# Moving the gelu and the sums of one pass behind other work, and three more idle products, in a two-layer S5, retention and convolution kernel

## The chip, the cores and the metric

The kernel runs on 1 core of a Trainium2 chip, as one program in one launch. The metric is the device time of an execution in microseconds (us), as the median of several runs. TensorE is called PE here, VectorE DVE, ScalarE ACT, GpSimd POOL and SyncE SP. SP issues nearly all transfers (DMAs), in order, so a transfer whose condition is not met holds up those behind it on SP.

## What is computed

The input x has 1024 frames of 1024 values, in float32. Two layers act on it, each as x + mixer(rmsnorm(x)), with a norm at the end.

```python
# layer 0
u, g_s5, q, k, v, g_ret = split(h @ w_in)
y = gelu(s5_mixer(u))                        # diagonal complex state space, chunks of 64
y = y * sigmoid(y @ glu_w + glu_b) * silu(g_s5)
r = retention(rope(q), rope(k), v)           # 8 heads, dk 64, dv 128; normalised per head
x = x + concat(y, r * silu(g_ret)) @ w_out
# layer 1
a, b, g = split(h @ w_in_c)
c = layernorm(causal_conv31(a * sigmoid(b)) + conv_b)
x = x + (silu(c) * silu(g)) @ w_out_c
out = rmsnorm(x)
```

## The kernel before, in words

Data lie with the features on the 128 partitions and the 1024 frames along the free axis, in two halves of 512. So a matrix of 1024 x 1024 values is eight blocks of 128 features. Every large product is made of three products of a rounded high part and a low part (`mm3`, lines 180 to 182: high weight by high x, high weight by low x, low weight by high x). Weights come in as float32, ACT casts the high part (line 170), and DVE or POOL subtracts it to get the low part (line 171).

`run` goes through three stages.

1. `layer0_front`. PE starts with idle products (lines 271 to 273): products of a matrix of ones, whose result nobody reads, as many as the constant WARM says (9). Meanwhile the first pieces of the weights and of x arrive, ACT makes the high part of x (line 295) and DVE the low part (line 296). Squares of x are summed over the blocks on DVE into `ssum` (line 268). The first GEMM, u0 and u1 (lines 310 to 318), runs over the eight blocks kb of the input dimension; then comes the GEMM of u2, and between its halves the sums over the features of `ssum` by 16 small products (line 443, `ss`). The remaining u blocks, the gates and the state space follow. The state space leaves its result in DRAM (`y_d`).
2. `retention`, a loop over 4 pairs of heads. Each pair makes its k and q (`ret_proj`; line 979 evacuates them as `kraw` and `qraw`, four transfers each swap their halves for the rotation, line 988), its values v (`ret_values`: for pairs 2 and 3, eight blocks v_0 to v_7 of 24 products, lines 1025 to 1027, each evacuated by ACT on line 1028), and its heads (`ret_heads`). A pass of y, `y_pass`, is done once in each pair, for the feature blocks k and k + 4.
3. `layer0_back_and_layer1`: the gated linear unit (GLU) on y, the output projection, the convolution, the last projection and the last norm.

PSUM has 8 banks; the pool that the large products share has three, so a new block of v waits for the evacuation of the block three before it.

The order of the instructions on each engine is decided by a scheduler, which runs a model of the timeline when the kernel is built. The source orders it in two ways: `issue_after(x)` adds an edge, so that what is made in it is ordered behind x; and a `yield` in a generator splits a step into parts which the caller starts at a place of its choice.

`y_pass(rq, pair)` is such a generator. For each of its two blocks it loads `yp` from `y_d` (line 878; one buffer, which the high parts of the same pass, `th`, also use), applies gelu on ACT (line 881, the first of each pass with a table load) into `yn` (two buffers) and stores that to `yn_d` (line 883). Four DVE operations, the sums (lines 888 to 891), then combine the halves of the two blocks in place. They are ordered behind `last_raw`, the last evacuation of k or q, and must wait for the stores to `yn_d`, whose data they overwrite. A `yield` follows. The last part casts each block to a high part `th` (line 895), subtracts it in place (line 896) and stores both to `t_d` (lines 897 and 898). These t_d sums, and similar sums of the GLU's weights (`glu_sums`, stored to `ws_d`), let the GLU use fewer products.

In `ret_heads`, k is transposed into `kt` (line 1066, DVE on 1068), kt times v gives the states' increments `kv` (line 1085), DVE runs the recurrence over the chunks into `S` (lines 1093 and 1095), PE makes the scores `sp` (line 1102), DVE multiplies them with the decay mask into `sc` (line 1108), and PE adds `ro` = q times S (line 1129) and sc times v (line 1134). The norm per head (lines 1143 to 1149), a transpose back (`rt`, line 1157) and the gate (line 1160) end the pair. The last of the four mask products is kept as `masked[1]`.

In the loop of `retention`, before the change, the first part of `y_pass` (loads, gelus, stores and sums) is started ahead of `ret_heads`, behind the `rs` of the pair before; in pairs 1 and 2 the rest (casts and stores to t_d) is started behind `masked[1]`. In pair 2 the second gelu is ordered behind `last_v`, the evacuation of the eighth value block; the first gelu has no such edge. In pair 3 all is started ahead of the heads.

Behind the pass of pair 3, the loads `y11f` and `y21f` (line 1191) bring the blocks of yn back for the GLU, and ACT casts them (line 1167, `y11h`).

Of the kernel before, what the change touches and what calls it, by code (L numbers as in the profile page):

```python
# [26 lines left out]
CONV_K = 31  # L27
MAGIC = 12582912.0
N0, HOLD = 5, 1
WARM = 9  # L30
RMM = 5
IDLE = 4
TWICE = ("wo", "cb", "ca", "cg")
# [18 lines left out]
class Trunk:  # L52
# [190 lines left out]
    def layer0_front(self, st):  # L243
# [27 lines left out]
        idle = self.bank("idle")  # L271
        for _ in range(WARM):
            nc.tensor.matmul(idle[:, :P], self.ones[:], self.ones[:], start=True, stop=True)
# [597 lines left out]
    def y_pass(self, rp, k):  # L871


        nc = self.nc
        yns = []
        for i, cb in enumerate((k, k + 4)):
            yt = rp.tile([P, 8, P], F32, name=f"yp_{cb}", tag="yp", bufs=1)
            nc.sync.dma_start(yt[:], self.y_d[cb].rearrange("i h g m -> (h g) i m"))
            yn = rp.tile([P, P, 8], F32, name=f"yn_{cb}", tag="ynt", bufs=2)
            with self.tc.issue_after(self.last_v.ins) if k == 2 and i else nullcontext():  # L880
                nc.scalar.activation(yn[:], yt[:].rearrange("p i m -> p m i"), AF.Gelu_apprx_tanh)
            yn = yn[:].rearrange("p m i -> p (m i)")
            nc.sync.dma_start(self.yn_d[cb * P:(cb + 1) * P], yn)
            yns.append(yn)
        (b11, b12), (b21, b22) = ((y[:, :HALF], y[:, HALF:]) for y in yns)
        v = nc.vector
        with self.tc.issue_after(self.last_raw.ins):
            v.tensor_tensor(b22, b22, b12, op=ALU.subtract)
            v.tensor_tensor(b12, b12, b11, op=ALU.subtract)
            v.tensor_tensor(b11, b22, b11, op=ALU.add)  # L890
            v.tensor_tensor(b21, b11, b21, op=ALU.subtract)
        yield
        for i in range(2):
            hi = rp.tile([P, T], F32R, name=f"th{i}_{k}", tag="yp", bufs=1)
            v.tensor_copy(hi[:], yns[i])
            v.tensor_tensor(yns[i].bitcast(F32R), yns[i], hi[:].bitcast(F32), op=ALU.subtract)
            nc.sync.dma_start(self.t_d[i, 0, k * P:(k + 1) * P], hi[:].bitcast(F32))
            nc.sync.dma_start(self.t_d[i, 1, k * P:(k + 1) * P], yns[i])
# [20 lines left out]
    def retention(self, st):  # L919
        nc, A = self.nc, self.A  # L920
        rp = self.rp = self.pool("ret", 1, stack=st)
        early = ExitStack()
        rq = self.rq = self.pool("retq", 1, stack=early, side="right")
        self.rk = rq.tile([P, 2, T], F32, name="ropek")
        nc.sync.dma_start(self.rk[:], A["rope_k"])
        self.g128 = rp.tile([P, 4], F32, name="g128")
        nc.sync.dma_start(self.g128[:], A["ret_g128"])
        ahead = None
        for pair in range(4):
            cur = list(ahead or self.ret_proj(pair))[-1]  # L930

            ahead = pair == 1 and self.ret_proj(pair + 1)
            if ahead:
                next(ahead)
            for g, tag in (((0, "swp"), (1, "raw")), (), ((3, "raw"),), ())[pair]:
                self.glu_sums(g, tag)
            if pair == 0:
                V = self.ret_values_wide()
            elif pair > 1:
                V = self.ret_values(pair)  # L940
            with ExitStack() as held:
                if pair:
                    held.enter_context(self.tc.issue_after(self.last_rs.ins))
                parts = self.y_pass(rq, pair)
                next(parts)
                if pair in (0, 3):
                    next(parts, None)

            def turned():
                if pair == 3:  # L950
                    early.close()
                    self.lp = self.pool("l1", side="right")
            self.ret_heads(pair, *cur, V, turned)

            if pair < 3:
                with self.tc.issue_after(self.masked[1].ins):
                    if pair == 0:
                        self.glu_sums(2, "swp")
                    else:
                        next(parts, None)  # L960

    def ret_proj(self, pair):
        nc, A, rp = self.nc, self.A, self.rp
# [48 lines left out]
    def ret_values(self, pair):  # L1012

        nc = self.nc
        wv = [self.wnext(f"v{pair}_{i}") for i in range(2)]
        vt = self.rp.tile([P, 8, 256], F32, name=f"v_{pair}", tag="v", bufs=2)
        for b in range(8):
            ps = self.bank(f"mm_v{pair}_{b}", aux=False)
            h, o = b // 4, (b % 4) * P
            for kb in range(KB):  # L1020
                xh, xl = self.xs[h][kb]
                i, k4 = kb // 4, kb % 4
                wh = wv[i][0][:].rearrange("p (k a) n -> p k (a n)", a=2)[:, k4, :]
                wl = wv[i][1][:].rearrange("p (k a) n -> p k (a n)", a=2)[:, k4, :]
                nc.tensor.matmul(ps[:, :256], xh[:, o:o + P], wh, start=kb == 0, stop=False)
                nc.tensor.matmul(ps[:, :256], xh[:, o:o + P], wl, start=False, stop=False)
                nc.tensor.matmul(ps[:, :256], xl[:, o:o + P], wh, start=False, stop=kb == KB - 1)
            self.last_v = nc.scalar.mul(vt[:, b, :], ps[:, :256], self.Rtok[:, b:b + 1])
        return lambda p, b, hh: vt[:, b, hh * P:(hh + 1) * P]

    def ret_values_wide(self):
# [700 lines left out]
```

## Time and profile before

| | us |
|---|---|
| median of 3 runs | 1191.57 |
| the runs | 1190.52, 1191.57, 1194.78 |
| the profiled execution | 1192.05 |
| its span in the trace | 1190.3 |
| PE busy | 1179.0 |
| DVE, POOL, ACT busy | 848.5, 657.8, 481.3 |

The span is what the trace shows, from the first instruction to the last. It is 1.75 us shorter than the time of the same execution. A row of the timeline reads: start, duration, engine, line and operation, result <- operands by their names without numbers, shapes and types, xcount of instructions that the row holds, and in brackets the idle time of the engine ahead of it, with what ended it. A product's duration reaches into the next one's, since products are pipelined: the pace is read from the starts. The waits give for each pair of waiter and releaser the total, the number and the longest. The stretches give, for a window of the span, the busy time of PE, PE's weight loads, DVE, ACT and POOL, each with its count, then the granted clock, the share of the DMA engines and what they moved.

### The profile page before, as it was taken

To read this page: it belongs to the slowest core of one execution; us is meant where nothing else is said; L and a number is where in the kernel's file an instruction comes from. 1 tells how busy PE (TensorE), PEld (TensorE's weight loads), DVE (VectorE), ACT (ScalarE), POOL (GpSimd) and SP (SyncE) were. 2 spreads that over 40 slices of the span, in tenths; PEclk is the share of its full clock that TensorE was granted. 3 is DMA by queue.
4 is the path that set the end of the run, shared out by engine and by line. 5 is a ranking of instruction groups with operands and counts; after the bars stand their busy time and mean duration, and the time that the engine had idled before them with its cause. 6 is when DMAs were issued, how large, how long until landed. Compare 5 with 4: busy or idle time off the path is not lost.

```text
span 1190.3 us, 17367 instructions
## 1 busy us (share of the span) xinstructions
PE 1179.0 (99%) x6366; PEld 988.1 (83%) x6366; DVE 848.5 (71%) x1452; ACT 481.3 (40%) x706; POOL 657.8 (55%) x448
## 2 busy tenths in 40 slices
PE   9999999999999999999999999999999999999997
PEld 7888888888888888899878888888888888888887
DVE  7975798777427459577769323599999799999533
ACT  6222233222232231333446323546535675434563
POOL 2059999988145354242573110688543567757653
PEclk9999999999999999999999999999999999999999
DMA  9244356555388566769998986756668554357773
GB/s 357 91 140 137 116 159 195 176 168 175 109 279 304 211 218 193 255 207 357 381 323 287 333 271 214 233 192 215 222 234 283 205 192 154 134 177 249 246 257 138
DMA packets 117638, 261.47 MB, mean 220 GB/s; under 512 B 10672, under 2 KB 42288, under 8 KB 116912
## 3 DMA queue, kind: packets, MB, share of 16 engines
q1 hardware_dynamic: 117408, 260.33, 64.7%
q8 instruction: 50, 0.82, 0.3%
q14 instruction: 36, 0.29, 0.1%
q10 hardware_dynamic: 144, 0.03, 0.0%
HBM read 181.48 MB, written 74.65 MB: 215 GB/s over the span
## 4 chain that ended last, share of the span: by engine, by line
PE 49%; DMA 3%; POOL 2%; issue 1%; SPq 0%; ACT 0%; DVE 0%; DVEq 0%; POOLq 0%; ACTq 0%
PE mm_wo L182 5%; PE mm_wo L181 5%; PE mm_wo L180 5%; PE mm_g L180 2%; PE mm_b L182 2%; PE mm_g L182 2%; PE mm_b L180 2%; PE mm_b L181 2%; PE mm_a L180 2%; PE mm_g L181 2%; PE mm_a L181 2%; PE mm_a L182 2%; PE mm_oc L181 2%; PE mm_oc L182 2%; PE mm_oc L180 2%; PE mm_glu L180 1%
## 5 line engine op out<-in xcount | busy, mean ns | idle before, releaser
L1415 DVE SCALAR_TENSOR_TENSOR cv<-u,convw,cv 128x512 f32<-128x512 f32 x398 | 273.6, 750 | 12.8 <-ACT cv L1401 10.5
L1395 POOL TENSOR_TENSOR tp<-tp,tp 128x512 f32<-128x512 f32 x64 | 83.0, 1297 | 43.6 <-ACT tp L1394 42.5
L180 PE MATMUL mm_g<-xh,wh_g 128*128 128x512 f32 x256 | 101.8, 398 | 0.0
L182 PE MATMUL mm_g<-xh,wl_g 128*128 128x512 f32 x256 | 100.1, 391 | 0.0
L181 PE MATMUL mm_g<-xl,wh_g 128*128 128x512 f32 x256 | 100.0, 391 | 0.0
L412 POOL TENSOR_TENSOR s1q<-s1q,s1q 128x512 f32<-128x512 f32 x12 | 17.8, 1481 | 76.8 <-ACT s1q L407 76.8
L1394 ACT ACTIVATE tp<-u,convw 128x512 f32<-128x512 f32 x64 | 45.4, 719 | 31.4 <-POOL tp L1395 31.1
L180 PEld LDWEIGHTS mm_g<-xh,wh_g 128*128 128x128 f32 x256 | 48.0, 188 | 11.7 <-issue 1.2
L182 PEld LDWEIGHTS mm_g<-xh,wl_g 128*128 128x128 f32 x256 | 48.0, 188 | 10.4
L181 PEld LDWEIGHTS mm_g<-xl,wh_g 128*128 128x128 f32 x256 | 48.1, 188 | 9.9 <-issue 0.4
L180 PE MATMUL mm_oc<-zh,wh_woc 128*128 128x512 f32 (+1 forms) x152 | 54.5, 364 | 0.0
L368 DVE TENSOR_TENSOR gt<-mm_g,R 128x512 f32<-128x512 f32 x32 | 21.9, 684 | 45.5 <-PE mm_g L182 45.5
L181 PE MATMUL mm_oc<-zl,wh_woc 128*128 128x512 f32 (+1 forms) x152 | 54.0, 357 | 0.3 <-POOL zl L1169 0.3
L182 PE MATMUL mm_oc<-zh,wl_woc 128*128 128x512 f32 (+1 forms) x152 | 53.8, 357 | 0.0
L171 POOL TENSOR_TENSOR wl_glu<-wf_glu,wh_glu 128x1024 fp32r<-128x1024 f32 x14 | 34.9, 2491 | 31.7 <-ACT wh_glu L170 25.1
L180 PE MATMUL mm_u<-xh,wh_u 128*128 128x512 f32 x128 | 51.3, 401 | 0.6 <-ACT wh_u L170 0.5
L181 PE MATMUL mm_u<-xl,wh_u 128*128 128x512 f32 x128 | 50.6, 395 | 0.0
L180 PE MATMUL mm_g<-h1h,wh_cg 128*128 128x512 f32 x128 | 50.4, 394 | 0.0
L180 PE MATMUL mm_b<-h1h,wh_cb 128*128 128x512 f32 x128 | 50.2, 392 | 0.0
L182 PE MATMUL mm_a<-h1h,wl_ca 128*128 128x512 f32 x128 | 50.2, 392 | 0.0
L182 PE MATMUL mm_u<-xh,wl_u 128*128 128x512 f32 x128 | 50.0, 395 | 0.0
L180 PE MATMUL mm_wo<-ysh,wh_wos 128*128 128x512 f32 x128 | 49.9, 390 | 0.0
(490 smaller groups left out, 3649.6 us busy)
## 6 DMA issues: line engine op xcount, KB each, us to landing
wf_g<-w_ab SPq DMA_DIRECT2D x16, 512.0 KB
wf_wos<-w_out SPq DMA_DIRECT2D x16, 512.0 KB
wf_wor<-w_out SPq DMA_DIRECT2D x16, 512.0 KB
wf_cb<-w_c SPq DMA_DIRECT2D x16, 512.0 KB
wf_ca<-w_c SPq DMA_DIRECT2D x16, 512.0 KB
wf_woc<-w_out_c SPq DMA_DIRECT2D x16, 512.0 KB
wf_v<-w_v SPq DMA_DIRECT2D x12, 512.0 KB
wf_cg<-w_c SPq DMA_DIRECT2D x11, 512.0 KB
```

The costliest lines, as they stand in the source:

```text
L171: lo[i].tensor_tensor(wl[:].rearrange(fl)[:, c], wf[:, c], h.bitcast(F32), op=ALU.subtract)
L180: nc.tensor.matmul(ps, wh[:, kb, :], xh, start=start, stop=False, **more)
L181: nc.tensor.matmul(ps, wh[:, kb, :], xl, start=False, stop=False, **more)
L182: self.last_mm = nc.tensor.matmul(ps, wl[:, kb, :], xh, start=False, stop=stop, **more)
L368: nc.vector.tensor_tensor(gt[:, c], ps[:], self.R[:, c], op=ALU.mult)
L412: nc.gpsimd.tensor_tensor(a, a, sq[:], op=ALU.add)
L1394: nc.scalar.mul(sk[:], u[:, k:k + HALF], cw[:, nb, k:k + 1])
L1395: gp.tensor_tensor(s0[:], s0[:], sk[:], op=ALU.add)
L1415: v.scalar_tensor_tensor(dst[:], *tap, accs_[i][:], op0=ALU.mult, op1=ALU.add)
```

## The change

WARM goes from 9 to 12. In `y_pass` for pair 2, the first gelu is ordered behind `mid_v`, the evacuation of the fifth value block (b == 4), and the second stays behind `last_v`. A new `yield` stands between the gelus and the sums. In `retention`, pairs 0, 1 and 3 call `next` once more, so that their order of parts stays; in pair 2 the sums and the casts are both started behind `masked[1]`, after `ret_heads` has been laid out. Lines of the new file lie two further down from `y_pass` on, and more behind it.

```diff
-WARM = 9
+WARM = 12
...
-            with self.tc.issue_after(self.last_v.ins) if k == 2 and i else nullcontext():
+
+            with self.tc.issue_after((self.last_v if i else self.mid_v).ins) if k == 2 else nullcontext():
                 nc.scalar.activation(yn[:], yt[:].rearrange("p i m -> p m i"), AF.Gelu_apprx_tanh)
             yn = yn[:].rearrange("p m i -> p (m i)")
             nc.sync.dma_start(self.yn_d[cb * P:(cb + 1) * P], yn)
             yns.append(yn)
+        yield
         (b11, b12), (b21, b22) = ((y[:, :HALF], y[:, HALF:]) for y in yns)
...
                 next(parts)
+                if pair != 2:
+                    next(parts)
                 if pair in (0, 3):
                     next(parts, None)
...
                     else:
-                        next(parts, None)
+                        for _ in parts:
+                            pass
...
             self.last_v = nc.scalar.mul(vt[:, b, :], ps[:, :256], self.Rtok[:, b:b + 1])
+            if b == 4:
+                self.mid_v = self.last_v
```

The scheduler orders everything anew. Beside the steps named, the order on the engines changes in these places. On PE the products of u0 and u1 for kb 2 to 5 are sorted by operand, one product of u2's second half goes ahead of the `ss` sums, and some products of k of pair 3 change places with the heads of pair 2. On ACT the cast of a weight block of v3 goes ahead of the gelu of yn_6, and that of the first GLU weight block ahead of the gelu of yn_7. On DVE the sums and casts of pair 2 are interleaved with the norm statistics behind the masks, and the second half of kraw_3 goes ahead of the last cast. On SP the store of yn_2 and the load of yp_6 go behind the gs1_3 and ropeq_3 loads, two ws_d stores, two yr_d stores and a grl load; the store of yn_6 goes behind the second grl load and a GLU weight load; the four kswp transfers of pair 3 go ahead of the load of yp_3; and the second pair of y11f loads directly follows the store of yn_7.

## The prediction

> **What bounds the kernel now.** I read the page first, then the stretches by engine, then TensorE's waits. The page:
>
> ```profile
> span 1190.3 us, 17367 instructions
> PE 1179.0 (99%) x6366; PEld 988.1 (83%) x6366; DVE 848.5 (71%) x1452; ACT 481.3 (40%) x706; POOL 657.8 (55%) x448
> ```
>
> TensorE (PE) is busy for all but 11.3 us of the span. The change takes no real product away, so it can only touch those 11.3 us, or the speed at which the products run. Where the idle lies, by stretches (the first figure after the length is PE's busy time):
>
> ```profile
> 0.00:10.00 10.00, 8.45 (x28) 7.24 (x29) 4.94 (x12) 6.24 (x10) 0.84 (x7) 1.00 0.79 293
> ...
> 60.00:460.00 400.00, 400.00 (x2479) 333.76 (x2479) 263.63 (x427) 109.55 (x167) 279.55 (x187) 1.00 0.57 183
> 460.00:480.00 20.00, 19.53 (x148) 18.34 (x147) 17.14 (x59) 7.04 (x11) 9.24 (x6) 1.00 0.70 210
> 480.00:520.00 40.00, 38.99 (x291) 34.35 (x290) 27.02 (x79) 9.40 (x13) 10.09 (x6) 1.00 0.71 246
> ...
> 1100.00:1190.30 90.30, 82.80 (x457) 70.72 (x455) 39.91 (x74) 47.38 (x76) 43.74 (x36) 0.98 0.62 214
> ```
>
> 7.5 us of the idle lie behind 1100, in the last norm, which the change does not touch. In reach are 1.55 us in the first 10, 0.47 in 460 to 480 and 1.01 in 480 to 520. PE's waits name their releasers:
>
> ```profile
> PE sp L1102 <- DVE S L1095: 0.6, 1, 0.6
> ...
> PE mm_u L180 <- ACT wh_u L170: 0.5, 1, 0.5
> PE ro L1129 <- DVE sc L1108: 0.4, 1, 0.4
> PE mm_v L1025 <- ACT v L1028: 0.3, 1, 0.3
> ```
>
> The second stands at the front; the others are pair 2, where the two moved steps are. So at most some 3 us of waits can go, a quarter per cent. More can come back than goes, because a new wait has no such ceiling.
>
> **Part 1, twelve idle products.** Each idle product is two rows (18 rows for nine), so the change adds six.
>
> ```profile
> 1.05 4.21 PE L273 MATMUL idle<-ones 128*128 128x128 f32 x18 [1.05 <-DVE mhalf L217]
> ...
> 5.76 0.80 PE L180 MATMUL mm_u<-xh,wh_u 128*128 128x512 f32 x1 [0.49 <-ACT wh_u L170]
> ...
> 6.12 0.42 DVE L171 TENSOR_TENSOR wl_u<-wf_u,wh_u 128x256 fp32r<-128x256 f32 x1
> ...
> 9.81 0.39 PE L180 MATMUL mm_u<-xh,wh_u 128*128 128x512 f32 x1
> ...
> 33.18 1.28 DVE L268 TENSOR_TENSOR ssum<-ss,sq 128x512 f32<-128x512 f32 x2
> ...
> 34.75 0.40 PE L182 MATMUL mm_u<-xh,wl_u 128*128 128x512 f32 x1
> 34.98 1.90 PE L443 MATMUL ss<-ones,ssum 128*128 128x64 f32 x16
> ```
>
> 18 rows take 4.21 us, 0.234 each, and end at 5.26; then comes the gap of 0.49. Between 5.76 and 9.81 stand nine real products, 4.05 us; from 9.81 to 34.75 stand 110, 24.94 us or 0.227 each. Nine at that pitch are 2.04, so the slow start costs 2.0 us. The granted clock of the stretch rounds to 1.00 and does not show it; the durations do.
>
> With 24 rows the idle work ends at 1.05 + 24 x 0.234 = 6.66, or earlier if the clock rises in it. The first operands have come by then (the wh_u cast releases the row at 5.76, wl_u ends at 6.54), so no gap is left. If the clock is full from there, the nine end at 6.66 + 2.04 = 8.70 in place of 9.81: 1.1 earlier. If it is not, the same nine at the old pace end 0.9 later. By the nearest row 4.2 us of idle products did not lift the clock, and 4.05 us of real ones behind them did; an unbroken 5.6 us lies above either, so I take the rise.
>
> What is late next is the token sums at 34.98: they need ssum, which DVE ends at 33.18 + 1.28 = 34.46, a slack of 0.52. I keep 0.45 of the 1.1. In the changed order one product of the next GEMM (0.23) moves ahead of the sums, into that new wait. **Front: -0.7**, bounds -1.3 (DVE earlier too) and +0.9.
>
> The Trainium skill, TensorE: Matmul & The Clock Gate, section Part 1: The HAM clock gate, says that the clock rises after one busy window of some 3.4 us, and that the window runs freely, so the point varies by run. The nine idle products here ran for 4.21 us without a rise, which agrees only if no whole window fell into them. By that rule alone 24 rows always hold a rise before 7.9, and the sum would again be what the ssum limit leaves.
>
> **Part 2, the first gelu behind the fifth value block.** ACT's order changes: today the gelu of yn_2, with its table load, stands between the evacuations of v2_0 and v2_1.
>
> ```profile
> 475.54 2.06 ACT L881 ACTIVATE yn<-yp 128x1024 f32<-128x1024 f32 x1
> ...
> 477.51 1.18 ACT L1028 ACTIVATE v<-mm_v,Rtok 128x256 f32<-128x256 f32 x3
> ...
> 478.01 0.39 PE L1025 MATMUL mm_v<-wh_v,xh 128*128 128x256 f32 x1 [0.32 <-ACT v L1028]
> ```
>
> The evacuation that frees v2_4's bank is held until 477.51, and PE shows 0.47 idle in 460 to 480, with a refill of about 0.1. The gelu leaves that place: **-0.58**. It goes behind v2_4; what queues behind it on ACT is the evacuation of v2_5, and with three banks that bank is needed only after v2_7, two blocks on, so I cost the new place at nothing; without that cover it would cost what it costs now, 0.5. Its store and the next yp load follow it on SP past gs1_3, ropeq_3, two ws_d stores and three head transfers, so the second gelu's store yn_6 also goes late.
>
> **Part 3, the sums behind the masked scores.** Now they stand on DVE between kt_2 and S_2. Pair 1, whose sums do not, is the yardstick:
>
> ```profile
> 453.25 0.39 PE L182 MATMUL mm_q<-xh,wl_q 128*128 128x512 f32 x1
> 453.57 1.04 PE L1102 MATMUL sp<-qrot,krot 64*128 64x128 f32 x13
> ...
> 455.33 2.05 PE L1134 MATMUL ro<-v,sc 128*128 128x128 f32 x16
> ...
> 497.96 0.69 DVE L888 TENSOR_TENSOR yn<-yn,yn 128x512 f32<-128x512 f32 x1 [6.41 <-DMA yn_d<-yn]
> ...
> 500.75 0.28 DVE L1093 COPY S<-kv 128x128 f32<-128x128 f32 x1
> ...
> 501.31 0.39 PE L180 MATMUL mm_k<-xh,wh_k 128*128 128x512 f32 x1
> 502.33 1.13 PE L1102 MATMUL sp<-qrot,krot 64*128 64x128 f32 x14 [0.64 <-DVE S L1095]
> ...
> 505.01 2.05 PE L1134 MATMUL ro<-v,sc 128*128 128x128 f32 x16
> ```
>
> DVE stands still 6.41 us, until the store of yn_6 has landed (the sums write in place over what is stored), then spends four sums of 0.73, and S starts only at 500.75. PE pays for it: 501.31 to 502.33 is 1.02 where pair 1 has 453.25 to 453.57, 0.32; 502.33 to 505.01 is 2.68 where pair 1 has 1.76. Together 0.70 + 0.92 = **-1.62**. That also holds the loss of small products at half pace, which is why it is above the 1.01 idle. With part 2: -2.2 by 510.
>
> **What is given back.** The same four sums now stand behind the masks, and the whole chain to pair 3's y pass behind them.
>
> ```profile
> 504.87 1.28 DVE L1108 TENSOR_TENSOR sc<-sp,retmask 128x512 f32<-128x512 f32 x2
> ...
> 513.03 1.20 DVE L896 TENSOR_TENSOR yn<-yn,th 128x1024 fp32r<-128x1024 f32 x1
> ...
> 514.68 0.38 SPq L878 DMA_DIRECT2D yp<-y_d  x1
> ...
> 517.19 2.50 SPq L988 DMA_DIRECT2D kswp<-kraw  x4
> ...
> 528.62 2.07 ACT L881 ACTIVATE yn<-yp 128x1024 f32<-128x1024 f32 x1 [5.20 <-issue]
> ...
> 531.52 0.84 ACT L1028 ACTIVATE v<-mm_v,Rtok 128x256 f32<-128x256 f32 x2
> ...
> 534.46 0.28 PE L1025 MATMUL mm_v<-wh_v,xh 128*128 128x256 f32 x1
> ...
> 542.26 0.62 ACT L1167 CAST y11h<-y11f 128x512 fp32r<-128x512 f32 x1 [1.55 <-DMA y11f<-yn_d]
> ...
> 543.31 0.38 PE L1025 MATMUL mm_v<-wh_v,xh 128*128 128x256 f32 x1
> ```
>
> From S at 500.75 to the last mask at 506.15 are 5.4 us; with S starting at about 497.0, when kv's first products are done, the masks end near 502.4. Then come the sums (2.9), the norm and cast work that today lies between 506.15 and 514.23 (8.1), and the second half of kraw_3 (0.7), which the new order puts ahead of the last cast, with some more norm work: about 515. On SP the four kswp transfers (2.5 by their row) and the t_d stores now stand ahead of pair 3's yp load: issued at about 518, in place of 514.68, **3.2 later**. From there the chain is yp, gelu yn_3, yp again (one buffer), gelu yn_7. That ends at 528.62 + 2.07 = 530.69 today, so near 533.9. The evacuation of v3_0 stands right behind it on ACT (the wh_glu0 cast now goes ahead of the gelu): about 534.3. Its bank is needed by v3_3, which PE reaches at 534.46 today and, 2.2 ahead, at 532.3. Today's slack is 534.46 - 531.95 = 2.5 us; it turns into a wait of 2.0. Allowing 0.1 for orders that fall luckier: **+1.9**.
>
> The next tight place, y11f2's cast at 542.26 ahead of the product at 543.31, gets easier: its load now directly follows yn_7's store on SP, not behind a qswp transfer. Nothing else in the order touches a wait later on; waits behind 549 start from PE's own events and move with it.
>
> **Sum.** -0.7 - 2.2 + 1.9 = -1.0: 1191.05 against the profiled execution's 1192.05 (span 1190.3 and 1.75 around it). That run lies 0.48 above the median of 1191.57, so I predict **1190.6**.
>
> **The rivals.**
> - **Slack keeps its gain.** The store of yn_6 gives no delay, the y chain is only 1 us late, and v3_0's evacuation stays ahead of PE: -0.7 - 2.2, or 1188.7. For it: my chain adds many rows. Against: the four sums alone move it by 2.9, and kswp comes on top.
> - **The y chain decides, slower than before.** Everything hangs on when yn_7's gelu ends. By my sum 533.9; at 534.9 the wait eats the whole gain, front included. One slow store does it: the sums need yn_6's store, which took 492.32 to 497.96 for its like today, and the yp load needs the hi tile's store. If yn_7 ends at 537 to 538, which a store of 3 us more gives, +2 to +3: 1193 to 1195.
> - **The idle products miss the clock.** PE then starts 0.9 later on products at the old pace, and the front is +0.5 to +0.9 in place of -0.7: 1192.0. [...]
> - **The front does nothing.** ssum comes no earlier and the extra product gains nothing, so only -0.3 of the middle is left: 1191.3.
>
> **Chances.** My case: 0.42. The same with a front that does nothing: 0.08. Gain kept: 0.17. Y chain slower than before: 0.25, of which 0.10 by more than 0.5% if the wait grows through y11f2 and the GLU operands as well. Clock missed: 0.08. 0.5% is 6 us, about what a measurement of this kernel can tell from no change, so all but the tail is within it. Faster by 6 us would need twice the idle that is in reach: 0.03, out of the kept gain's share. The range goes from the kept gain with the front's far bound (1192.05 - 0.48 - 2.2 - 1.3 = 1188.1) to the late chain's 1195. Over the two signs, I give 0.65 to a time below 1191.57; the likeliest case alone spans 1189.5 to 1191.8.
>
> **What would show it.** Right: 24 rows of idle products ending by 6.7 and real products at 0.227 pitch before 8; the token sums waiting for ssum; no PE wait for v at v2_4 or for S at sp; L888's group (two lines lower in the new file) behind the masks; pair 3's first yp near 518, and a new PE wait on v's evacuation of about 2 us near 532. Wrong: yp issued before 516 (gain kept) or behind 521 (slower); that wait above 4 us; a PE wait at kt_3, y11h or the GLU products that is not there now; or products at 0.43 pitch up to 9.8 again.

## The result, and the profile after

| | median, us | runs | ratio to before, 95% interval |
|---|---|---|---|
| before | 1192.55 | 13 | |
| changed | 1197.42 | 13 | 1.0042 [1.0032, 1.0051] |

The changed kernel is 0.42% slower, some 5 us. The prediction had forecast a gain of 1 us, at 1190.6, with a range of 1188.1 to 1195; 1197.42 lies above that range. The loss is below the half per cent that the prediction took as the least that can be told from no change, but its interval is clear of zero. Its profiled execution took 1197.96, with a span of 1196.2; before had 1192.05 and 1190.3. The page of the changed kernel:

```profile
span 1196.2 us, 17380 instructions
...
PE 1180.2 (99%) x6372; PEld 989.6 (83%) x6372; DVE 851.8 (71%) x1452; ACT 481.6 (40%) x706; POOL 654.6 (55%) x448
```

PE is busy 1.2 longer than before and idle for 16.0 in place of 11.3. Its waits (total, times, longest):

```profile
PE mm_v L1030 <- ACT v L1033: 5.1, 1, 5.1
PE mm_glu L180 <- ACT mm_glus L1249: 1.1, 1, 1.1
...
PE mm_glu L180 <- DVE gu L1282: 0.5, 1, 0.5
PE v L792 <- DMA U<-u_d: 0.4, 1, 0.4
...
PE ss L443 <- DVE ssum L268: 0.3, 1, 0.3
```

The waits at sp, at ro and at v2_4 are gone. In their place stands one wait of 5.1 for v's evacuation, in pair 3. (In the names, yp_3 and yn_3 belong to the first block of pair 3's pass and yn_7 to the second; yn_2 and yn_6 are those of pair 2, and th0_2 and th1_2 its two high parts; v3_3 is the fourth value block of pair 3. Lines from `y_pass` on are two further down in the new file, from `ret_proj` on five, in `ret_heads` and behind seven.)

To see where the time went, I counted the real products on PE in both traces and compared the starts of those with the same number; for `ss` it is the first of these products in each trace, which the changed order puts one place later. Idle products are not counted.

| place | before | after | difference |
|---|---|---|---|
| first real product | 5.76 | 6.19 | +0.43 |
| tenth | 9.81 | 8.40 | -1.41 |
| first of the token sums `ss` | 34.98 | 34.74 | -0.24 |
| state space, first product that needs `U` of one group | 183.94 | 184.00 | +0.06 |
| last product of v2_3, just ahead of v2_4 | 477.42 | 476.93 | -0.49 |
| v2_4 | 478.01 | 477.05 | -0.96 |
| end of pair 2's heads | 509.86 | 507.01 | -2.85 |
| v3_3, first product | 534.46 | 536.99 | +2.53 |
| v3_3, 23rd product | 537.10 | 541.84 | +4.74 |
| GLU | 581.99 | 586.53 | +4.54 |
| GLU | 630.96 | 636.78 | +5.82 |
| last product | 1183.45 | 1189.38 | +5.93 |

So 2.9 are gained between 184 and 510. Of these, 0.5 come ahead of v2_4, where no step was moved, and 2.4 at v2_4, sp and ro, where the moved steps were to bring 2.2. Then 5.4 are lost in one place, 2.2 right behind it, and 1.3 in the GLU. The lost 5.4, followed back in the timeline of the changed kernel:

```profile
495.45 0.29 DVE L1100 COPY S<-kv 128x128 f32<-128x128 f32 x1 [4.96 <-PE kv L1092]
...
500.58 1.29 DVE L1115 TENSOR_TENSOR sc<-sp,retmask 128x512 f32<-128x512 f32 x2 [0.80 <-PE sp L1109]
...
511.57 2.38 POOL L171 TENSOR_TENSOR wl_v<-wf_v,wh_v 128x1024 fp32r<-128x1024 f32 x1 [9.47 <-ACT wh_v L170]
...
512.18 2.33 DVE L897 CAST th<-yn 128x1024 fp32r<-128x1024 f32 x1 [0.76 <-DMA t_d<-th]
514.53 0.32 SPq L899 DMA_DIRECT2D t_d<-th  x1
...
520.00 0.53 SPq L878 DMA_DIRECT2D yp<-y_d  x1
...
525.88 2.10 ACT L882 ACTIVATE yn<-yp 128x1024 f32<-128x1024 f32 x1
...
528.42 0.39 SPq L878 DMA_DIRECT2D yp<-y_d  x1
...
534.65 1.92 ACT L882 ACTIVATE yn<-yp 128x1024 f32<-128x1024 f32 x1 [5.73 <-issue]
536.48 1.19 ACT L1033 ACTIVATE v<-mm_v,Rtok 128x256 f32<-128x256 f32 x3
536.99 0.58 PE L1030 MATMUL mm_v<-wh_v,xh 128*128 128x256 f32 x1 [5.13 <-ACT v L1033]
537.36 0.41 PE L1031 MATMUL mm_v<-wl_v,xh 128*128 128x256 f32 x1
...
542.26 0.28 PE L1030 MATMUL mm_v<-wh_v,xh 128*128 128x256 f32 x1
```

Read it from the top. S starts as soon as kv is there, and the last mask ends at 501.87. The sums and casts follow; th1_2's cast waits 0.76 for the one yp buffer, which the store of th0_2 holds, and then takes 2.33 instead of 0.67. The yp load of pair 3 is issued at 520.00 (514.68 before), the second gelu ends at 536.57 (530.69 before), the three evacuations behind it run in a row, and PE waits from 531.86. The products behind the wait start 0.213 apart instead of 0.120, until 542.26. The stretches show the clock (the last three columns are granted clock, DMA share and GB/s):

```profile
531.00:535.00 4.00, 0.85 (x8) 0.65 (x6) 0.00 (x0) 0.35 (x1) 0.40 (x1) 1.00 0.99 268
535.00:539.00 4.00, 2.02 (x9) 2.02 (x10) 0.00 (x0) 3.82 (x6) 0.00 (x0) 0.55 0.96 362
539.00:543.00 4.00, 4.00 (x24) 4.00 (x23) 2.72 (x3) 1.15 (x3) 2.52 (x2) 0.59 0.97 302
543.00:547.00 4.00, 4.00 (x36) 4.00 (x35) 4.00 (x8) 1.07 (x4) 0.00 (x0) 1.00 0.53 197
```

### The profile page after: what moved, and what is told of

It reads as the page before. It is cut to its first block, busy times and chain, and to the rows that moved or that the text cites. A ratio compares the mean times of both kernels' runs of the same rounds, so it can differ in the third digit from the quotient of the medians.

```text
span 1196.2 us, 17380 instructions
## 1 busy us (share of the span) xinstructions
PE 1180.2 (99%) x6372; PEld 989.6 (83%) x6372; DVE 851.8 (71%) x1452; ACT 481.6 (40%) x706; POOL 654.6 (55%) x448
## 4 chain that ended last, share of the span: by engine, by line
PE 48%; DMA 3%; issue 2%; POOL 1%; DVE 1%; ACT 1%; DVEq 0%; SPq 0%; POOLq 0%
PE mm_wo L180 5%; PE mm_wo L182 5%; PE mm_wo L181 5%; PE mm_g L180 2%; PE mm_b L182 2%; PE mm_b L181 2%; PE mm_g L182 2%; PE mm_g L181 2%; PE mm_a L182 2%; PE mm_a L180 2%; PE mm_b L180 2%; PE mm_a L181 2%; PE mm_oc L181 2%; PE mm_oc L182 2%; PE mm_oc L180 2%
## 5 line engine op out<-in xcount | busy, mean ns | idle before, releaser
L182 PE MATMUL mm_b<-h1h,wl_cb 128*128 128x512 f32 x128 | 49.9, 390 | 0.0
L181 PE MATMUL mm_b<-h1l,wh_cb 128*128 128x512 f32 x128 | 49.9, 390 | 0.0
L182 PE MATMUL mm_g<-h1h,wl_cg 128*128 128x512 f32 x128 | 49.9, 390 | 0.0
```

Of the source, the lines that this page charges most:

```text
L181: nc.tensor.matmul(ps, wh[:, kb, :], xl, start=False, stop=False, **more)
L182: self.last_mm = nc.tensor.matmul(ps, wl[:, kb, :], xh, start=False, stop=stop, **more)
```

## The experiments

The theory from the trace, here the late chain: the sums behind the masks make the casts of pair 2 late, these hold the single yp buffer, and through it pair 3's y pass and all that stands behind its second gelu on ACT. Rivals: the front did it; the place of the evacuation behind the gelu did it, and not the chain; the halved clock did it; the place of the yp load in SP's queue did it, as the prediction had it. All of these runs together, with before run beside them (the kernel before was itself 1191.4 to 1192.6 in these groups, so runs of different groups are compared by their ratios):

| run | what it is | median (before beside it) | ratio [95%] |
|---|---|---|---|
| e1_warm | before, twelve idle products | 1190.04 (1191.40) | 0.9990 [0.9980, 0.9999] |
| e2_y_only | changed, nine | 1194.67 (1192.63) | 1.0020 [1.0008, 1.0031] |
| e3_gelu_only | before, first gelu moved | 1198.76 (1192.63) | 1.0057 [1.0043, 1.0072] |
| e4_sums_only | before, sums moved | 1195.96 (1191.40) | 1.0033 [1.0021, 1.0045] |
| e5_third_v | changed, yn_7's gelu behind v3_2 | 1198.57 (1191.40) | 1.0060 [1.0044, 1.0077] |
| e6_fill | changed, wait filled | 1196.79 (1191.40) | 1.0040 [1.0027, 1.0052] |
| e8_yp_ahead | changed, yp_3 ahead of two kswp | 1198.38 (1192.63) | 1.0048 [1.0032, 1.0065] |
| e9_th_swp | changed, th_2 in the swp buffers | 1190.04 (1192.63) | 0.9986 [0.9974, 0.9998] |
| e10_pool_behind | changed, one POOL step moved | 1194.71 (1191.54) | 1.0031 [1.0018, 1.0043] |
| e11_swp_pool | e9 and e10 together | 1188.69 (1191.54) | 0.9974 [0.9964, 0.9984] |
| e12_before_swp | before, th_2 in swp, twelve | 1188.81 (1191.54) | 0.9974 [0.9965, 0.9983] |
| e13_swp_nine | e9 with nine | 1189.88 (1191.54) | 0.9991 [0.9979, 1.0003] |
| e14_before_swp_nine | before, th_2 in swp | 1191.09 (1192.54) | 0.9983 [0.9970, 0.9995] |
| b2_before | before, one more profiled execution | 1194.71 (1192.54) | |
| b3_before | before, one more profiled execution | 1192.59 (1192.54) | |

### The parts alone

**e1_warm.** Only the constant:

```diff
-WARM = 9
+WARM = 12
```

> The kernel before with twelve idle products alone. By the prediction's front: -0.7 against before, the first real products at a pitch of 0.227 from about 6.4 instead of 9.8. By the ledger of the two traces (the lead of 1.4 at 9.8 is down to 0.3 behind the token sums at 35 and gone at 184, where PE waits for a load of u in the state space): 0 within 0.5. If the front were what makes the changed kernel slow, +3 or more.

Measured: 0.9990, about -1.2. It neither slows the kernel nor is it quite nothing. The lead at the tenth product is 1.43, at `ss` 0.22: as in the changed kernel (1.41 and 0.24). So the front is not the cause.

**e4_sums_only.** The changed kernel without the `mid_v` edge and with nine idle products.

```diff
...
-            with self.tc.issue_after((self.last_v if i else self.mid_v).ins) if k == 2 else nullcontext():
+            with self.tc.issue_after(self.last_v.ins) if k == 2 and i else nullcontext():
...
```

> Nine idle products, the first gelu where it was (between the evacuations of v2_0 and v2_1), only the sums and casts of pair 2 behind the masked scores. If the late chain to pair 3's second gelu comes from the sums' place (the late-chain theory): the wait of v3_3 for v's evacuation is there with 3 to 5.5 us, and the kernel is 3 to 6 slower than before. If it comes from the first gelu's place: no such wait, a gain of 1 to 2.

Measured: 1.0033, about +4, within the forecast of the first case. PE waits twice for v's evacuation:

```profile
PE mm_v L1030 <- ACT v L1033: 3.5, 2, 2.4
```

Only one of the two is in pair 3: 2.4 at v3_3, at 536.20, below the 3 to 5.5 of the forecast. The other, 1.1 at 478.85, is the wait at v2_4, which stays since the first gelu has its old place. The sums alone make the late chain: yp_3 is issued at 519.42 here.

**e3_gelu_only.** The other half: before, with `mid_v` and its edge.

> The kernel before with only the first gelu moved behind the fifth value block; sums ahead of the heads, nine idle products. The store of yn_6 then goes out some 2 later than before (494.5 in the changed trace against 492.3), and the sums ahead of S wait for it: v2_4's wait gone, -0.6; the waits at sp and ro longer by 1 to 2.5; then pair 3's chain at most 2 late, which its slack of 2.5 takes. +0.5 to +2 against before. If the gelu's place makes the late chain by itself: a wait at v3_3 of 3 or more, +4.

Measured: 1.0057, about +6, the worst of the parts, and both cases were wrong on size. The store of yn_6 goes out at 496.84 and not at the 494.5 that I had taken from the changed trace, and the sums ahead of S wait for it. (In the nine traces with both moved steps this store goes out anywhere from 494.5 to 498.5, so the one trace was a poor source for it.) PE then waits 1.0 at sp, 2.4 at v3_3, 2.7 and 2.3 in the GLU:

```profile
PE mm_glu L180 <- ACT sg L1244: 2.7, 1, 2.7
PE mm_v L1025 <- ACT v L1028: 2.4, 1, 2.4
PE mm_glu L180 <- DVE mm_gluz L1289: 2.3, 1, 2.3
...
PE sp L1104 <- DVE sc L1110: 1.0, 1, 1.0
```

The two moved steps belong together, then: the gelu's new place makes yn_6 late, and only sums that come later can stand that. Either of them makes pair 3 late.

**e2_y_only.** The changed kernel with WARM back at 9.

> The changed kernel with nine idle products. If the front's gain is small and adds to the rest: 0.5 to 1.5 above the changed kernel, with the same wait of 5 at v3_3. If the longer wait is partly the front's doing (PE comes earlier and so waits longer for a chain that starts from DVE and the stores): the same as the changed kernel within 0.5.

Measured: 1.0020, some 2.6 faster than the changed kernel, which neither case had. In its timeline the POOL step and the cast of th1_2 stand the other way round:

```profile
511.34 0.69 DVE L897 CAST th<-yn 128x1024 fp32r<-128x1024 f32 x1
...
511.59 2.71 POOL L171 TENSOR_TENSOR wl_v<-wf_v,wh_v 128x1024 fp32r<-128x1024 f32 x1 [9.47 <-ACT wh_v L170]
```

Here th0_2's store landed in time for the cast to start 0.25 ahead of POOL. The cast takes 0.69, POOL 2.71; in the changed trace POOL was first by 0.61, and the cast took 2.33. yp_3 is issued at 517.53, and the wait at v3_3 is 2.6 instead of 5.1. e10 takes this up.

### What the wait consists of

**e5_third_v.** The evacuations of v3_0 to v3_2 ahead of the late gelu on ACT.

```diff
-            with self.tc.issue_after((self.last_v if i else self.mid_v).ins) if k == 2 else nullcontext():
+            behind = (self.last_v if i else self.mid_v) if k == 2 else self.third_v if k == 3 and i else None
+            with self.tc.issue_after(behind.ins) if behind else nullcontext():
...
+            if b == 2:
+                self.third_v = self.last_v
```

> The changed kernel with the second gelu of pair 3 ordered behind the evacuation of v3_2, so that v3_0 to v3_2 are evacuated ahead of it; their operands are there by 532, and the gelu's data only at 534.6. Late-chain theory (the evacuation behind the gelu is the price, 5.2 of waiting and 2.2 of halved clock behind it): no wait at v3_3, no half clock, some 7 less than the changed kernel, 1 to 3 under before. Rival (what is late is the chain itself, and its next user takes the wait): a wait of 3 or more at y11h or later, and 0 to 3 less than the changed kernel.

Measured: 1.0060; nothing gained. The wait at v3_3 is gone, and other waits take its place:

```profile
PE kv L1095 <- DVE kt L1078: 2.7, 1, 2.7
PE mm_glu L180 <- ACT sg L1252: 1.5, 1, 1.5
...
PE mm_glu L180 <- DVE mm_gluz L1297: 1.0, 1, 1.0
```

kt_3 stands behind pair 3's sums on DVE, and these wait for yn_7's store. Up to 547 PE was 2.5 ahead of before; at 627 it was 4.0 behind. This fits the rival of this run, that the lateness of the chain costs, whoever waits for it first. But it does not prove it, since the scheduler gave SP another order as well. In the changed kernel yn_7's store goes out as soon as its gelu has ended at 536.57:

```profile
536.60 0.32 SPq L884 DMA_DIRECT2D yn_d<-yn  x1
...
544.64 0.32 SPq L1198 DMA_DIRECT2D y21f<-yn_d  x1
```

In e5_third_v it stands behind two y11f and two grl loads and goes out 2.8 behind the end of its gelu at 536.69:

```profile
539.51 0.38 SPq L885 DMA_DIRECT2D yn_d<-yn  x1
```

So a part of the lateness that kt_3 meets is this run's own.

**e6_fill.** Idle products in the wait, to keep the clock up:

```diff
...
+            if pair == 3 and b == 3:
+                bk = self.bank("idle3")
+                with self.tc.issue_after(last.ins):
+                    for _ in range(22):
+                        fill = nc.tensor.matmul(bk[:, :P], self.ones[:], self.ones[:], start=True, stop=True)
...
```

> The changed kernel with 22 idle products (44 rows of 0.117, 5.15 us) put on PE between the last product of v3_2 and the first of v3_3, where PE waits 5.2 us. It leaves the wait's cause as it is and only keeps PE busy. If the wait halves the clock for the 25 products behind it: no products at a pitch of 0.213 there, and 2.2 less than the changed kernel. If the slow products have another cause: the same as the changed kernel.

Measured: 1.0040 against the changed kernel's 1.0042: no gain. The first case was right about the clock and not about the time:

```profile
531.88 5.07 PE L1028 MATMUL idle<-ones 128*128 128x128 f32 x44
...
537.18 0.38 PE L1037 MATMUL mm_v<-wh_v,xh 128*128 128x256 f32 x1 [0.23 <-ACT v L1040]
...
554.42 0.50 PE L180 MATMUL mm_glu<-y11h,wh_glu 128*128 128x512 f32 x1 [1.70 <-ACT v L1040]
```

The products behind the fill run at full pace, so the wait does lower the clock. But PE then waits 1.7 ahead of the GLU, for an evacuation of v on ACT. This evacuation stands behind the cast of a y21f block, and the y21f loads go out late:

```profile
550.35 1.03 SPq L1205 DMA_DIRECT2D y21f<-yn_d  x2
```

In the changed kernel the first of them go out at 544.64, ahead of all the stores to t_d of pair 3's pass; here three of these stores go first. So the edit did not leave all else alone: the fill brought another order on SP, with a wait of its own. The run shows that the wait halves the clock. What the slow stretch is worth in the changed kernel's own order it does not show.

### What makes the chain late

**e8_yp_ahead.** The load of yp_3 laid out right behind pair 2's casts, which puts it ahead of the last two kswp transfers on SP.

```diff
...
+                        if pair == 2:
+                            self.yp_ahead = self.yp_load(rq, 3)
```

> The changed kernel with the load of yp_3 moved ahead of the last two kswp transfers on SP, nothing else in that stretch. If the place in SP's queue is what makes yp_3 late (the prediction's step): issued 1.3 earlier, near 518.6, and the wait of v3_3 shorter by as much. If the single buffer is (th1_2's store must land first): at most 0.4 earlier, and the same time within 0.5.

Measured: 1.0048; nothing gained.

```profile
518.56 0.38 SPq L873 DMA_DIRECT2D yp<-y_d  x1
518.99 1.79 SPq L999 DMA_DIRECT2D kswp<-kraw  x2
...
526.84 2.09 ACT L886 ACTIVATE yn<-yp 128x1024 f32<-128x1024 f32 x1
```

The issue did come 1.44 earlier, as the queue's theory had it: th1_2's store had landed by 518.56. But the gelu started at 526.84, 0.96 later than in the changed kernel, and PE's wait at v3_3 grew to 6.9. The load went out among the kswp transfers and took 7.0 to its gelu's table load, instead of 4.6. So the place on SP did set the issue, and issuing earlier did not help. How much later the load comes in is known from this one execution alone, which took 1200.98, 2.6 more than its kernel's median.

**e9_th_swp.** The buffer itself: th0_2 and th1_2 go to the two buffers of the tag swp, which kswp and qswp use, and no longer hold the one yp buffer.

```diff
-            hi = rp.tile([P, T], F32R, name=f"th{i}_{k}", tag="yp", bufs=1)
+            hi = rp.tile([P, T], F32R, name=f"th{i}_{k}", tag="swp" if k == 2 else "yp", bufs=2 if k == 2 else 1)
```

> The changed kernel with the high parts th0_2 and th1_2 in the two swp buffers in place of the single yp buffer. So the load of yp_3 no longer waits until th1_2 is stored (issued at 514.5, landed near 519.6 by the changed trace), but only for its place on SP. Late-chain theory with the single buffer as its link: yp_3 is issued by 510, the gelu of yn_7 ends before 532, no wait at v3_3 and no half clock; 5 to 7 less than the changed kernel. Rival (the y pass of pair 3 is held by the yn buffers or the order on ACT instead): the gelu of yn_7 still ends behind 535, at most 2 less.

Measured: 0.9986, about 7 less than the changed kernel, as the theory had it. The load of yp_3 is issued at 496.22, right behind yn_6's store:

```profile
496.22 0.43 SPq L878 DMA_DIRECT2D yp<-y_d  x1
...
527.68 2.08 ACT L882 ACTIVATE yn<-yp 128x1024 f32<-128x1024 f32 x1 [5.28 <-DMA yp<-y_d]
```

The gelu of yn_7 ends at 529.76, and no wait at v3_3 is listed, nor one for mm_glus. The gelu and the sums stand where the change put them, so it is not their place that costs, but the buffer through which they reach pair 3.

**e10_pool_behind.** POOL's subtraction for the second v3 block behind krot_3; from 210 us on, the order on every engine is that of the changed kernel but for this one pair on POOL.

```diff
...
+            with self.tc.issue_after(self.last_raw_turn.ins) if name == "v3_1" else nullcontext():
```

> The changed kernel with one thing moved: POOL's subtraction for the second weight block of v3 goes behind both halves of krot_3, so that it no longer runs from 511.6 to 513.9 while DVE casts th1_2. In the changed trace that cast takes 2.33 from 512.18, in the trace with nine idle products 0.67 from 511.34, just ahead of POOL. If the two block each other: the cast is back at 0.7, the load of yp_3 some 1.7 to 2.5 earlier (near 518), the wait of v3_3 at 2.5 to 3.5 in place of 5.2, and the time near that of nine idle products, 2 to 3 less than the changed kernel. If the cast was slow for another reason: 2.3 again and the same time.

Measured: 1.0031 against 1.0042. By the ratios that is 1.3 less, with intervals that overlap; by the medians, 2.7.

```profile
511.39 0.69 DVE L898 CAST th<-yn 128x1024 fp32r<-128x1024 f32 x1 [0.20 <-DMA t_d<-th]
...
516.45 2.39 POOL L172 TENSOR_TENSOR wl_v<-wf_v,wh_v 128x1024 fp32r<-128x1024 f32 x1
...
517.58 0.53 SPq L879 DMA_DIRECT2D yp<-y_d  x1
```

Cast 0.69, yp_3 2.4 earlier, the wait at v3_3 2.9: in the trace all is as the first case had it. Of the 2.4, 1.6 are the cast that no longer meets POOL; the other 0.8 come from the buffer, which th0_2's store sets free earlier in this trace. What that is worth in time is less sure, as the two figures above show.

### Whether the moved steps are worth anything

Four kernels out of the edits above: e11 has the swp line of e9 and the POOL line of e10, e13 the swp line and nine idle products, both in the changed kernel; in the kernel before, e12 has the swp line and twelve idle products, and e14 the swp line alone.

> Both cures together: the high parts of pair 2 in the swp buffers, and POOL's subtraction moved as in the run beside it. The chain already ends in time with the first cure alone, so the second should give nothing more: the time of that kernel within 1 (some 2 to 3 under before). If slack in the chain were still worth time: 1 to 2 less.

> The kernel before with twelve idle products and the high parts of pair 2 in the swp buffers, but gelu and sums where they were. It has no late chain, so the buffers alone should give nothing: -0.5 to -1.5 against before, as twelve idle products alone. If the moved gelu and sums are worth their 2.9 once the chain is cured, this kernel is 1 to 2 slower than the cured changed kernel; if not, the same.

> The changed kernel with the high parts of pair 2 in the swp buffers and nine idle products. If the front has no worth of its own (the lead is spent at the token sums and at the load of u): the same as with twelve within 1. If it has: 1 to 1.5 slower than with twelve. In its trace the first products may be fast from 6 or slow up to 9.8: with nine idle products both were seen.

e11 is the fastest version, with e12: 0.9974 both, 1188.69 and 1188.81, better than either kernel of the change. By the ratios e11 is 1.4 below e9, as the second case of its expectation had it, though the intervals overlap. In the timeline of e11's SP queue the load of yp_3 goes out at 494.90, and the second gelu of pair 3 has its result stored from 526.64:

```profile
494.90 0.43 SPq L879 DMA_DIRECT2D yp<-y_d  x1
...
519.88 0.43 SPq L879 DMA_DIRECT2D yp<-y_d  x1
...
526.64 0.32 SPq L885 DMA_DIRECT2D yn_d<-yn  x1
```

e12 has the gelu and the sums in their old places and is just as fast. So I was wrong in that expectation on both counts: the second buffer helps the kernel before too, and with it the moved steps bring nothing. The pair with nine idle products says the same: e13 (moved) 0.9991 [0.9979, 1.0003], e14 (not moved) 0.9983 [0.9970, 0.9995]. e13 lies 0.6 above e9, the same within 1, and e14 lies 2.0 below before: the first case for both. Where the second buffer saves time in the kernel before, whose traces have no wait at v3_3, is open.

Why they bring nothing was the last question. In e12 and e1, which keep the sums ahead of S, there is no wait at sp. I suspected that the profile of before had caught one slow store, and profiled before twice more.

> The kernel before, unchanged, profiled once more. If the waits that the prediction counted as gain (0.47 at v2_4, and 1.0 at sp and ro behind the 6.4 that the sums wait for the store of yn_6) belong to every execution: the store lands 5 or more behind its issue and S starts near 500.5 again. If they were a slow landing of that one execution, as the trace with twelve idle products alone suggests (3.3 from issue to landing, S at 496.9): no wait at sp above 0.3.

> The kernel before, unchanged, profiled a third time, for the same question as the run beside it.

> The kernel before with the high parts of pair 2 in the swp buffers and nothing else; nine idle products. If the second buffer is what makes the cured kernels faster: 1.5 to 3 under before, as with twelve idle products. If the twelve idle products are: the same as before within 1.

At v2_4 the suspicion held: neither trace lists a wait for v's evacuation there, so the 0.58 that the prediction counted for it is not there in every execution. At sp and ro it fell. The store of yn_6 and the first sum in the timeline of one of them, b3_before:

```profile
491.42 0.32 SPq L883 DMA_DIRECT2D yn_d<-yn  x1
...
497.11 0.69 DVE L888 TENSOR_TENSOR yn<-yn,yn 128x512 f32<-128x512 f32 x1 [6.45 <-DMA yn_d<-yn]
```

5.7 from issue to the first sum; 5.3 in b2_before, 5.6 in before, 5.4 in e14_before_swp_nine. PE's waits at sp and ro are 0.7 and 0.4, 0.3 and 0.4, 0.6 and 0.4, 0.4 and 0.4. In the two kernels with twelve idle products and the sums in place it is 3.3 and 3.7:

```profile
490.82 0.32 SPq L883 DMA_DIRECT2D yn_d<-yn  x1
...
494.10 0.69 DVE L888 TENSOR_TENSOR yn<-yn,yn 128x512 f32<-128x512 f32 x1 [4.03 <-DMA yn_d<-yn]
```

(e1_warm). So in these six traces the counted wait belongs to the kernel with nine idle products, and goes by itself with twelve. The store is the same, at the same place of the same queue, and the sums can start 2 us sooner behind it. One thing differs in the traces: the four transfers ahead of it, two stores to ws_d and two loads of grl, go out from 486.82 to 490.69 in before, which leaves 1.6 up to the store, and from 482.79 to 487.63 in e1_warm, which leaves 3.2. That less is under way when the store goes out could be the reason; it was not tried alone. It is not the front's lead: b3_before had its front as early and its store as slow. The cause stays open.

Single traces differ elsewhere too: in the GLU PE waits 2.1 for POOL's wl_glu in b2_before, 0.8 in b3_before, and in before, which is the same kernel, no such wait is listed.

## Why the prediction was wrong, point by point

**The front: -0.7 forecast, nothing left by 184.** The clock rose as forecast: the tenth product starts at 8.40, forecast 8.70.

```profile
1.05 5.46 PE L273 MATMUL idle<-ones 128*128 128x128 f32 x24 [1.05 <-DVE mhalf L217]
...
8.40 0.39 PE L180 MATMUL mm_u<-xh,wh_u 128*128 128x512 f32 x1
```

The cap was there too (`ss` waits 0.3 for ssum), at -0.24 for the sums themselves. What was missing is a second cap: the state space waits 0.4 for a load of u, and the rest is gone. That cap is not in every execution: e1_warm's trace has no such wait and is 0.35 ahead at this place. By the ratios of e1 to before and of e12 to e14 the twelve are worth 1 or so all the same, which is more than this lead.

The rise itself depends on the execution. Of eight profiled executions with nine idle products four had slow products up to 9.7 or later, and four were at full pace by 7.2; all nine with twelve were by then. The margin was thin: in four of these nine the idle products still ran at half pace when they ended at 6.5. The Trainium skill, TensorE: Matmul & The Clock Gate, section Part 1: The HAM clock gate, has a window that runs freely and warm-up points that vary by run; the traces agree on the variation.

**Pair 2: -2.2 forecast, -2.4 measured from v2_4 on.** Right against the execution of before that was profiled. But e1_warm, with both steps in their old places, has none of these waits and gains about as much at the same places of its trace (2.25 from the end of v2_3 to the end of the heads, against 2.36); so the gain is not the moved steps' alone, and e11 against e12 shows no gain from them in time. One reading was wrong: the prediction put the excess of 1.62 over 1.01 down to small products at half pace. The products of ro behind the wait start 0.11 apart, as in pair 1, and the granted clock is 1.00.

**What is given back: +1.9 forecast, +5.4 measured. Here the prediction failed.** Its mechanism was the right one: kswp ahead of yp_3, the gelu of yn_7 late, v3_0's evacuation behind it, v3_3's wait. Its size was not. By terms:

- The masks were to end near 502.4; they ended at 501.87. Near, but in part by luck: S started at 495.45 and not at 497.0, and from there to the last mask it took 6.4 and not 5.4.
- yp_3 was to be issued at 518; it was at 520.00. The cast of th1_2 was taken at its old 0.67 and took 2.33: 1.7 of the 2.0. It also waited 0.8 for the buffer, which the sum did not have. The prediction counted what DVE had to do, and not what POOL did at that time. e10 shows the price.
- From there to the end of yn_7's gelu the forecast had 15.9, near the 16.0 of before; it took 16.6. The first load was quicker, the second slower (6.2 from issue to gelu against 4.8). Together 536.57 in place of 533.9.
- PE was to reach v3_3 at 532.3; it had gained more and was there at 531.7.

2.7 and 0.6 on top of the forecast wait of 2.0 are 5.3, about the 5.4 that were lost. The rival on the slow side named just this, "Everything hangs on when yn_7's gelu ends", with 534.9 as its turning point. The gelu ended 1.7 behind that, and the prediction gave this case 0.25. The rival's own reason, one slow store, covers little of it: the sums started right behind the last mask, with no wait for yn_6's store, and th0_2's store cost the 0.8 above. And for an end at 537 to 538 it had +2 to +3, where 536.57 came with +5. Two of the listed signs of being wrong came true: the wait above 4, and a wait at the GLU's products that was not there before.

**The clock behind the wait: not in the sum.** 25 products at 0.213 in place of 0.120 are 2.3. The sum took a wait at its length, with nothing for what runs behind it. e6_fill shows that the wait is the cause of the slow stretch; what that stretch alone is worth is not shown.

**"Waits behind 549 start from PE's own events and move with it": wrong, by 1.3.** PE waits 0.5 and 1.1 in the GLU, 0.6 before. The wait of 1.0 to 1.1 for mm_glus stands in the four kernels (changed, e2, e4, e10) in which ten products of yt1 go ahead of y22's, and in no other. I had overlooked this move: it stands in no list of changed orders ahead of the result, and the prediction said that nothing else in the order touches a wait later on. It wasn't tried alone.

**What I did not see at all** is that the slack of 2.5 at v3_0 was the only place that I priced, while kt_3, the casts of y11 and the GLU's evacuations hang on the same chain. e5 took the first user away, and others waited in its place, though with yn_7's store later than in the changed kernel. How much of the time each user would have asked for by itself is not shown; e9, which brings the whole chain forward, gives back all of it.

## What to carry to other kernels

When a step is moved to take a wait out of one stage, follow the buffer that the step fills and empties, up to the next user of that buffer in the next stage: here one shared buffer let 2.9 us of gain be followed by nearly 9 of loss, and a second buffer gave more than the move. Look at a delayed chain's lateness against all of its users and not at the slack of the first alone: in e5 and e6 the time that was taken out of the first wait came back at others, even if part of that was due to the new order of the scheduler. And when a step is moved on one engine, look at what its neighbour runs at the new time.

## What the runs showed of the hardware

- A DVE cast (128 x 1024, float32 to fp32r) and a POOL subtraction of the same size block each other. The one that starts first runs at its own length, the other is held: cast 0.67 to 0.69 alone, 2.33 when POOL began 0.61 earlier (it ended 0.56 behind POOL), 2.68 when POOL began 0.26 earlier; POOL 2.38 alone, 2.71 when the cast began 0.25 earlier. The subtraction on DVE is held as well, 3.11 against 1.22 in e9. The Trainium skill, SBUF — State Buffer, section SBUF: two separate sides, calls the port pair that the two share an exclusive lock, held for a whole instruction by whoever starts first; these rows agree with it.
- A wait of PE can halve the clock, and its length alone does not decide. After 5.1 the products ran at half pace for 5.3, after 6.9 (e8) for 3.6; after 2.6 (e2) they ran at full pace for 0.8 and then at half for 3.4; after 2.4 the clock fell in e4 and not in e3, and after 3.5 (e13) they stayed at full pace. The Trainium skill, TensorE: Matmul & The Clock Gate, section Part 1: The HAM clock gate, has the clock fall after an idle window of some 3.4. The waits of 2.4 and 2.6 are shorter than that and the clock fell; if such windows decide, a mostly idle one is enough.
- In e8 a load issued 1.4 earlier, among other transfers, was used 1 later: 7.0 from its issue to its gelu's table load in place of 4.6, with the DMA engines busy to a share of 0.9 to 1.1 in both. This is one execution of each.
